# Two-layer encoder trunk: small parameters in two transfers, tables behind the first tokens, one norm placed late, softmax factors as reductions, residual rows requested half a tile sooner

## The chip, the cores and the metric

The kernel runs on one core of a Trainium2 chip. The core has a matrix engine (TensorE, "PE" in the profile; its weight loads are "PEld"), a vector engine (VectorE, "DVE"), a scalar engine for activations (ScalarE, "ACT"), a general engine (GpSimd, "POOL") and an engine that here only issues transfers (SyncE, "SP"). Each engine works through its own list of instructions in a fixed order and waits on semaphores for the others. Working memory is SBUF (128 partitions); matrix products land in eight PSUM banks. The metric is the device time of one execution in microseconds, the median of several runs.

## The reference

The input `x` has 2048 tokens of 1024 values, in float32, and goes through two layers.

```python
def even_layer(...):
    h = rms_norm(x, norm_g); proj = h @ w_in          # 1024 -> 3328
    aq, ak = apply_rope(rms_norm(aq), cos, sin), apply_rope(rms_norm(ak), cos, sin)
    ya = sliding_window_sink_attention(aq, ak, av, a_sinks) * silu(ag)
    yb = chunked_relbias_attention(rms_norm(bq), rms_norm(bk), bv, b_rel) * silu(bg)
    return x + concatenate([ya, yb]) @ w_out
def odd_layer(...):
    h = rms_norm(x, norm_g); q, k, v, gate = split(h @ w_in)   # 4 x 1024
    lam = exp(sum(lq1*lk1)) - exp(sum(lq2*lk2)) + lambda_init
    # per head, with the chunk-causal mask:
    a = softmax(q1 @ k1.T / 8) - lam * softmax(q2 @ k2.T / 8); o = a @ v
    o = rms_norm(o, subln_g) * (1 - lambda_init)
    return x + (o * silu(gate)) @ w_out
```

Beside the large weights there are many small parameters: norm gains of 64 values, eight sinks, four lambda vectors of 64 values, one gain of 128 values, and a table of relative biases of which the far ones are one value per head. The cosine and sine tables are worked out on the host and passed in.

## The kernel before

**Precision.** A product is taken as three matmuls with each operand split into a high and a low part (`mm3`, lines 212 to 217). So each weight chunk is copied to its high part by ACT (line 314), and POOL (at the very start also DVE) subtracts to get the low part (line 319). Hidden rows are split in the same way after their transposes (lines 347 and 348).

**Tiling.** Tokens go in 4 blocks of 512, each of 4 tiles of 128. `_project` runs once per layer, in two halves of two blocks. For each half, `hidden` is called for both blocks: it loads a tile of x (line 264), takes its mean square on ACT (line 333), the root on ACT and DVE (`rstd`, lines 205 to 209), scales the tile on DVE (line 338), transposes it on PE (line 343) and splits it. Then column groups of 512 are projected for both blocks. Tiles of x come from a pool with the tag `xt`, three buffers in layer 0 and four in layer 1. `mix0` is layer 0's attention with its output projection (`out_tile`, line 553 adds the residual), `mix1` is layer 1's.

**Start.** After the first block's `hidden`, `tables()` (line 272) calls `parameters` (line 154): fourteen small transfers on SP's queue, most of them broadcasts to 128 partitions, the four lambda vectors into a tile of the tag `xt`. Then it loads cosine and sine, in pieces of 32 values, and makes the four rotary tables on DVE (`rope_tables`, lines 187 to 195).

**Layer 1's attention.** For each head and block, `scores` makes rows of scores, at most 512 columns at a time (lines 977 and 978), their maximum (981) and exponentials with their sums (984). When a row has several chunks (nb > 1), lines 993 to 999 bring the chunks to one maximum and one sum, and line 1002 makes the factor of the second softmax, lambda in it. Then `combine` scales the second map on ACT (1016), the first on POOL (1017) and adds them on POOL (1018). `values` transposes the result (1032), copies it out of PSUM on DVE (1034) and multiplies with v (1036) into one PSUM bank (`pO`). `gate` copies that bank into a tile of the tag `ot` (1060). `projected` is the output projection; `out_begin` (1195) takes an `ot` tile for the residual rows and asks for them (1198), `out_end` adds them (1210) and stores (1211). The tag `ot` has four buffers.

**Order.** The program is traced in one order; a planner with a cost model then lays out each engine's list: of what is ready it takes what was traced first, and gives buffers of a pool as they come free. `issue_after(i)` makes what is traced inside it follow instruction i on i's engine only. `pace` weaves scores, values and side work (gates, output projection) by shares.

## Time and profile before

| what | us |
|---|---|
| median of 3 runs | 2771.64 (2765.45 to 2773.63) |
| the profiled execution's own time | 2771.11 |
| its span, first to last instruction | 2769.3 |
| PE busy | 2681.2 |
| DVE busy | 1768.0 |
| ACT busy | 1595.9 |
| POOL busy | 1438.4 |

The span is 1.8 us shorter than that execution's time. Layer 0's projections fill the first 600 us, its attention lasts to about 1160 us, layer 1's projections to about 1730 us, and the rest is layer 1's attention with its output projection. Matmuls overlap, so a row's length is more than the step from one to the next. A time in square brackets behind a row is the idle time of the engine before it, and what ended it.

### The profile page before, as it was taken

What the parts mean: (1) busy time and instruction counts of PE and PEld (TensorE: products, weight loads), DVE (VectorE), ACT (ScalarE), POOL (GpSimd) and SP (SyncE); (2) the same over time, 40 slices, a digit from 0 to 9 for tenths busy, and PEclk for the clock granted to TensorE, in tenths of its full rate; (3) what the DMA queues carried; (4) which work ended last, traced back from release to release, by engine and by line L of the source; (5) the groups of instructions that cost most, each with busy time, mean ns of one, the idle gap of its engine ahead of it and who ended that gap; (6) DMA issues with size and microseconds to landing.
All of it is one profiled execution on the core that took longest, in us unless ns stands there. A gap on an engine that the chain in (4) does not pass through costs nothing.

```text
span 2769.3 us, 43201 instructions
## 1 busy us (share of the span) xinstructions
PE 2681.2 (97%) x13384; PEld 2159.7 (78%) x13384; DVE 1768.0 (64%) x4397; ACT 1595.9 (58%) x3975; POOL 1438.4 (52%) x1595
## 2 busy tenths in 40 slices
PE   7999999999999999999999999999999999898999
PEld 6888888888788888788887888777777776676776
DVE  7642285337777777447833773478887787777772
ACT  5443544357867766333343332588887777776771
POOL 3651255245535354326553552467776666767661
PEclk9999999999999999999999999999999999999999
DMA  5774338557766656655486545887666656454542
GB/s 159 243 241 147 112 124 285 186 177 229 231 209 181 181 176 203 188 180 145 130 273 214 123 130 186 267 256 256 201 220 212 201 179 201 124 188 142 165 130 93
DMA packets 336373, 518.43 MB, mean 187 GB/s; under 512 B 36368, under 2 KB 128272, under 8 KB 336144
## 3 DMA queue, kind: packets, MB, share of 16 engines
q1 hardware_dynamic: 331536, 507.30, 58.2%
q10 hardware_dynamic: 4608, 8.39, 0.8%
q8 instruction: 106, 1.74, 0.3%
q14 instruction: 123, 1.01, 0.1%
HBM read 358.56 MB, written 157.02 MB: 186 GB/s over the span
## 4 chain that ended last, share of the span: by engine, by line
PE 80%; DVE 5%; ACT 4%; DMA 3%; issue 2%; POOL 1%; SPq 0%; ACTq 0%; DVEq 0%; POOLq 0%
PE cO L1036 8%; PE p1mm L215 6%; PE p1mm L216 6%; PE p1mm L217 6%; PE cS L977 4%; PE cS L978 4%; PE ctr L1032 4%; PE p0mm L217 3%; PE p0mm L216 3%; PE p0mm L215 3%; PE mom L215 2%; PE mom L217 2%; PE mom L216 2%; PE cG L215 2%; PE cG L216 2%; PE cG L217 2%
## 5 line engine op out<-in xcount | busy, mean ns | idle before, releaser
L984 ACT ACTIVATE cP<-cS,cnm 128x512 f32<-128x512 f32 (+3 forms) x640 | 395.4, 624 | 144.6 <-DVE cnm L981 131.8
L981 DVE TENSOR_REDUCE cnm<-cS 128x1 f32<-128x512 f32 (+3 forms) x640 | 373.5, 601 | 47.5 <-PE cS L978 41.3
L1018 POOL TENSOR_TENSOR cP<-cP,cP 128x512 f32<-128x512 f32 (+1 forms) x320 | 356.8, 1142 | 18.4 <-ACT cP L1016 18.3
L1017 POOL TENSOR_SCALAR cP<-cP,crl,cel 128x512 f32<-128x512 f32 (+3 forms) x288 | 209.9, 742 | 246.0 <-DVE crl L999 112.4
L319 POOL TENSOR_TENSOR p0wL<-p0ws,p0wH 128x256 fp32r<-128x256 f32 x264 | 192.6, 765 | 268.9 <-ACT p0wH L314 255.4
L215 PE MATMUL p1mm<-p1wH,p1hH 128*128 128x512 f32 x768 | 300.4, 393 | 0.8 <-ACT p1hH L347 0.8
L217 PE MATMUL p1mm<-p1wH,p1hL 128*128 128x512 f32 x768 | 300.1, 391 | 0.0
L216 PE MATMUL p1mm<-p1wL,p1hH 128*128 128x512 f32 x768 | 299.3, 390 | 0.0
L1036 PE MATMUL cO<-cpt,cv 128*128 128x512 f32 (+3 forms) x640 | 285.8, 532 | 9.1 <-DVE cpt L1034 8.7
L977 PE MATMUL cS<-ck,cqd 128*128 128x512 f32 (+3 forms) x640 | 261.1, 412 | 6.5 <-ACT cP L984 5.4
L1034 DVE COPY cpt<-ctr 128x512 f32<-128x512 f32 (+1 forms) x320 | 190.9, 605 | 101.3 <-PE ctr L1032 97.7
L215 PE MATMUL p0mm<-p0wH,p0hH 128*128 128x512 f32 (+1 forms) x640 | 238.6, 375 | 9.2 <-ACT p0wH L314 4.5
L216 PE MATMUL p0mm<-p0wL,p0hH 128*128 128x512 f32 (+1 forms) x640 | 238.7, 375 | 0.0
L217 PE MATMUL p0mm<-p0wH,p0hL 128*128 128x512 f32 (+1 forms) x640 | 237.4, 372 | 0.1
L978 PE MATMUL cS<-ck,cql 128*128 128x512 f32 (+3 forms) x640 | 232.8, 368 | 0.0
L1032 PEld LDWEIGHTS ctr<-ident,cP 128*128 128x128 f32 x1088 | 137.4, 141 | 118.0 <-issue 60.7
L319 POOL TENSOR_TENSOR p1wL<-p1ws,p1wH 128x512 fp32r<-128x512 f32 x112 | 153.2, 1392 | 139.1 <-ACT p1wH L314 113.4
L1016 ACT ACTIVATE cP<-cP,cc 128x512 f32<-128x512 f32 (+1 forms) x320 | 189.3, 654 | 17.1 <-DVE cc L1002 16.1
L1032 PE MATMUL ctr<-ident,cP 128*128 128x128 f32 x1088 | 175.6, 273 | 4.8 <-POOL cP L1018 4.1
L784 POOL TENSOR_SCALAR mPB<-mPB,mbr 128x640 f32<-128x640 f32 (+4 forms) x128 | 92.9, 740 | 150.6 <-DVE mbr L781 105.9
L215 PEld LDWEIGHTS p1mm<-p1wH,p1hH 128*128 128x128 f32 x768 | 144.3, 188 | 29.8 <-ACT p1hH L347 1.2
L217 PEld LDWEIGHTS p1mm<-p1wH,p1hL 128*128 128x128 f32 x768 | 144.2, 188 | 29.7
(315 smaller groups left out, 6919.0 us busy)
## 6 DMA issues: line engine op xcount, KB each, us to landing
ck<-ck SPq DMA_DIRECT2D x144, 256.0 KB, 4.6
cw<-wg SPq DMA_DIRECT2D x64, 512.0 KB, 5.3
p1ws<-in_od_w_in_dram SPq DMA_DIRECT2D x56, 512.0 KB, 3.9
p0ws<-in_ev_w_in_dram SPq DMA_DIRECT2D x48, 512.0 KB, 4.6
cv<-v SPq DMA_DIRECT2D x72, 256.0 KB, 4.2
cqd<-qH SPq DMA_DIRECT2D x32, 512.0 KB, 6.5
cql<-qL SPq DMA_DIRECT2D x32, 512.0 KB, 7.2
mks<-bk SPq DMA_DIRECT2D x24, 512.0 KB, 6.8
```

The lines of the kernel that those rows point to most:

```text
L215: mm(ps, aH, bH, start=first, stop=False)
L216: mm(ps, aH, bL, start=False, stop=False)
L217: mm(ps, aL, bH, start=False, stop=last)
L319: low.tensor_tensor(l[:, cs], ws[:, k, cs], f32(h[:, cs]), ALU.subtract)
L977: mm(ps, qd[:, m, js], kt[:, :wd], start=True, stop=False)
L978: self.anchor = mm(ps, ql[:, m, js], kt[:, :wd], start=False, stop=True).ins
L981: nc.vector.tensor_reduce(nm[:, m, z:z + 1], ps, AX.X, ALU.max, negate=True)
L984: exp = nc.scalar.activation(chunks[z][:, :wd], ps, AF.Exp, bias=nm[:, m, z:z + 1], accum_out=acc).ins
L1017: nc.gpsimd.tensor_scalar(p1, p1, rl[:, 0:1], e1, ALU.mult, ALU.mult)
L1018: nc.gpsimd.tensor_tensor(p1, p1, p2, ALU.add)
L1032: nc.tensor.transpose(turned[:, (j - j0) * P:(j - j0 + 1) * P], us[j][kt // 4][:, kk:kk + P], self.ident)
L1036: mm(O[:, j0 * P:], v, T[:, :wd], start=(kt == 0), stop=(kt == nkt - 1), skip_group_check=True)
```

## The change

It touches five places.

1. All gains, sinks, column parameters and the far biases are put into one array `given` of 128 rows on the host and come in one transfer; the four lambda vectors come in a second one. The fourteen transfers, and the one for the far biases in `mix0`, become two. Cosine and sine are laid out on the host as SBUF holds them, so that a partition gets one piece of 512 values.
2. In layer 0 `tables()` is put inside `issue_after(self.split)`: the DVE instructions of parameters and tables follow the last split of the first block's hidden rows.
3. In layer 1, first half, the second block's roots and scalings (DVE) follow the last residual addition of layer 0.
4. In `scores` the factors are kept in eight fixed tiles f with the slots sum, exponential, reciprocal, and (1, lambda factor). The maximum over chunks is written once per chunk by a reduction over a repeated view, and differences, the sum and the factor c2 become reductions along a slot axis. The number of DVE instructions for a row with several chunks stays six.
5. `projected` asks for the next output tile's residual rows when half of the present tile's products are issued.

```diff
@@ parameters
-        for n, g in zip(("ev_a_q_norm", "ev_a_k_norm", "od_q_norm", "od_k_norm"), norms):
-            nc.sync.dma_start(g, a[n].to_broadcast([P, HD]))
-        for i in range(2):
-            nc.sync.dma_start(gq[i * HD:(i + 1) * HD], a["ev_b_q_norm"].rearrange("o d -> d o"))
-            nc.sync.dma_start(gk[i * HD:(i + 1) * HD], a["ev_b_k_norm"].rearrange("o d -> d o"))
+        nc.sync.dma_start(g, a["given"])
         nc.vector.scalar_tensor_tensor(self.b_gain, gq, -0.125, gk, ALU.mult, ALU.mult)
-        nc.sync.dma_start(self.sink, a["ev_a_sinks"].to_broadcast([P, 8]))
-        for i, n in enumerate(("q1", "k1", "q2", "k2")):
-            nc.sync.dma_start(lv[:, i, :], a["od_lambda_" + n].to_broadcast([P, HD]))
+        nc.sync.dma_start(tmp[:, 0:4 * HD], a["lambdas"])
...
-        nc.sync.dma_start(self.sub, a["od_subln"].rearrange("o d -> d o"))
@@ tables
-            nc.sync.dma_start(self.cos, a["cos"].rearrange("(t p) d -> p t d", p=P))
-            nc.sync.dma_start(self.sin, a["sin"].rearrange("(t p) d -> p t d", p=P))
+            nc.sync.dma_start(self.cos.rearrange("p t d -> p (t d)"), a["cos"])
+            nc.sync.dma_start(self.sin.rearrange("p t d -> p (t d)"), a["sin"])
@@ hidden
-                r = self.rstd(sm, ss, 1, 1.0 / D, n + "x")
...
+                with tc.issue_after(behind) if behind is not None else nullcontext():
+                    r = self.rstd(sm, ss, 1, 1.0 / D, n + "x")
+                    for c in range(0, D, step):
+                        cs = slice(c, c + step)
+                        nc.vector.scalar_tensor_tensor(xt[:, cs], xt[:, cs], r, g_in[:, cs], ALU.mult, ALU.mult)
...
-                    nc.vector.tensor_tensor(oL, ps3, f32(oH), ALU.subtract)
+                    self.split = nc.vector.tensor_tensor(oL, ps3, f32(oH), ALU.subtract).ins
@@ _project
             if layer == 0 and not tabs:
-                tables()
-            h.append(hidden(blocks[1], 1))
+                with tc.issue_after(self.split):
+                    tables()
+            h.append(hidden(blocks[1], 1, behind=self.added if layer and not half else None))
@@ _mix1
+        for i in range(8):
+            f = fc.tile([P, 4, 2, 4], F32, tag=f"f{i}", name=n + f"f{i}")
+            nc.gpsimd.memset(f[:, 3, 0, :], 1.0)
+            nc.scalar.activation(f[:, 3, 1, :], f[:, 3, 0, :], AF.Copy, scale=self.nlam)
+            factors.append(f)
@@ scores
-                    nc.vector.tensor_reduce(top, nm[:, :, :nb], AX.X, ALU.min)
-                    nc.vector.tensor_tensor(below, nm[:, :, :nb], top.unsqueeze(2).to_broadcast([P, 2, nb]), ALU.subtract)
+                    nc.vector.tensor_reduce(nt[:, 1, :, :nb], again(nm[:, :, :nb], nb), AX.X, ALU.min, negate=True)
+                    nc.vector.tensor_reduce(below, nt[:, :, :, :nb].rearrange("p i m z -> p m z i"), AX.X, ALU.add)
                     nc.scalar.activation(e[:, :, :nb], below, AF.Exp, scale=-1.0)
-                    nc.vector.tensor_reduce(pe, el[:, :, :nb, :], AX.X, ALU.mult)
-                    nc.vector.tensor_reduce(l, pe, AX.X, ALU.add)
-                nc.vector.reciprocal(rl, l)
+                    nc.vector.tensor_reduce(pe, slots(0, 2), AX.X, ALU.mult)
+                    nc.vector.tensor_reduce(l[:, :, :nb], again(pe, nb), AX.X, ALU.add)
+                    nc.vector.reciprocal(rl[:, :, :nb], l[:, :, :nb])
+                else:
+                    nc.vector.reciprocal(rl[:, :, :1], la[:, :, :1])
                 c2 = small("c2", 4)[:, :nb]
-                if nb > 1:
-                    nc.vector.tensor_scalar(c2, e[:, 1, :nb], rl[:, 1:2], self.nlam, ALU.mult, ALU.mult)
-                else:
-                    nc.vector.tensor_scalar(c2, rl[:, 1:2], self.nlam, None, ALU.mult)
+                nc.vector.tensor_reduce(c2, slots(1 if nb > 1 else 2, 4)[:, 1], AX.X, ALU.mult)
@@ projected
-                    xr, ps, to = out_begin(b, j, c)
+                    tiles.pop(0)
+                    xr, ps, to = out_begin(b, j, c, xr=ready.pop())
                     for k in range(KT):
                         out_step(b, j, k, ps, room)
+                        if k == KT // 2:
+                            ready.append(residual(b, *tiles[0]) if tiles else None)
```

More of the change, by code (lines that the diff above doesn't have):

```diff
@@ L147, in constants @@
         nc.scalar.activation(self.ones, self.ident, AF.Copy, bias=1.0, scale=0.0)
-        self.small = [t(*x) for x in (
-            ("ev_a_q_norm", [P, HD]), ("ev_a_k_norm", [P, HD]), ("od_q_norm", [P, HD]), ("od_k_norm", [P, HD]),
-            ("bq_g", [P, 1]), ("bk_g", [P, 1]), ("b_gain", [P, 1]), ("sink", [P, 8]), ("nsink", [P, 8]),
-            ("nlam", [P, 1]), ("sub", [P, 1]),
-        )]
+        self.given = t("given", [P, 4 * HD + 19])
+        self.b_gain, self.nsink, self.nlam, self.sub = (
+            t(*x) for x in (("b_gain", [P, 1]), ("nsink", [P, 8]), ("nlam", [P, 1]), ("sub", [P, 1]))
+        )
     def parameters(self, tmp):
@@ L322, in weights_by, with hidden @@
                 yield
-        def hidden(b, i, between=(), early=None):
+        def hidden(b, i, between=(), early=None, behind=None):
             hH, hL = hidden_tile("H", i), hidden_tile("L", i)
@@ L936, in _mix1 @@
         hx = pool("hx", 3)
+        fc = pool("fc", 1)
+        factors = []
+        for i in range(8):
[3 more added lines that the diff above has]
+            factors.append(f)
         NS, NTR, NO, NM = self.BANKS1
@@ L1193, in gates, with residual @@
                 move()
-        def out_begin(b, j, c, pl=None, tag="S"):
+        def residual(b, j, c):
             rows, cols = slice((b * NTB + j) * P, (b * NTB + j + 1) * P), slice(c * 512, (c + 1) * 512)
@@ L1198, in out_begin @@
             nc.sync.dma_start(xr, self.x1[rows, cols])
+            return xr
+        def out_begin(b, j, c, pl=None, tag="S", xr=None):
+            rows, cols = slice((b * NTB + j) * P, (b * NTB + j + 1) * P), slice(c * 512, (c + 1) * 512)
+            xr = xr or residual(b, j, c)
             if b < NB - 1:
```

47 lines of the change are left out of this document (28 added, 19 removed).

## The prediction

> **What bounds the kernel now.** I read the page first, its busy times and its chain:
>
> ```profile
> PE 2681.2 (97%) x13384; PEld 2159.7 (78%) x13384; DVE 1768.0 (64%) x4397; ACT 1595.9 (58%) x3975; POOL 1438.4 (52%) x1595
> PE 80%; DVE 5%; ACT 4%; DMA 3%; issue 2%; POOL 1%; SPq 0%; ACTq 0%; DVEq 0%; POOLq 0%
> ```
>
> PE sets the end: idle for 2769.3 - 2681.2 = 88.1 us. The change takes no matmul away, so it can only win from these 88 us and from time in which PE runs at a lower clock after a pause. Next I read who made PE wait:
>
> ```profile
> PE p0trh L343 <- DVE p0xt L338: 9.6, 2, 7.5
> PE cO L1036 <- DVE cpt L1034: 8.7, 6, 3.8
> PE p0mm L215 <- ACT p0wH L314: 4.5, 1, 4.5
> PE com L215 <- DVE cxr L1210: 4.4, 2, 3.2
> PE mom L215 <- DVE mxr L553: 3.2, 1, 3.2
> ```
>
> Of the first row, 7.5 us is the wait for the very first tile, which no part of the change touches. The other 2.1 us and the four rows below (20.8 us) are where the five edits work. Last I read the timeline of each engine around these waits, and the clock in stretches.
>
> **Part 1 and 2, the start.** Here are POOL, SP, DVE, ACT and PE from 8 to 56 us, and the stretch 20 to 28 us (columns: stretch, length, busy time of PE, PEld, DVE, ACT, POOL with counts, granted clock, DMA share, GB/s).
>
> ```profile
> 8.69 3.41 POOL L319 TENSOR_TENSOR p0wL<-p0ws,p0wH 128x256 fp32r<-128x256 f32 x4 [7.39 <-ACT p0wH L314]
> 13.22 0.47 SPq L165 DMA_DIRECT2D bk_g<-in_ev_b_k_norm_dram  x1
> 13.86 0.45 SPq L308 DMA_DIRECT2D p0ws<-in_ev_w_in_dram  x1
> 18.59 2.79 SPq L278 DMA_DIRECT2D p0sin<-in_sin_dram  x1
> 19.08 0.16 DVE L166 SCALAR_TENSOR_TENSOR b_gain<-bq_g,bk_g 128x1 f32<-128x1 f32 x1 [4.41 <-DMA bk_g<-in_ev_b_k_norm_dram]
> 20.20 1.15 ACT L314 ACTIVATE p0wH<-p0ws 128x512 fp32r<-128x512 f32 x2 [5.21 <-DMA p0ws<-in_ev_w_in_dram]
> 20.89 0.79 PE L215 MATMUL p0mm<-p0wH,p0hH 128*128 128x512 f32 x1 [4.51 <-ACT p0wH L314]
> 20.00:28.00 8.00, 7.09 (x25) 5.83 (x26) 7.96 (x14) 4.85 (x10) 2.45 (x2) 0.57 0.92 169
> 24.03 0.68 DVE L187 TENSOR_TENSOR p0tqC<-p0cos,ev_a_q_norm 128x512 f32<-128x512 f32 x1
> 37.35 0.15 DVE L174 SCALAR_TENSOR_TENSOR nlam<-p0tmp 128x1 f32<-128x1 f32 x1
> 37.52 24.63 SPq L264 DMA_DIRECT2D p0xt<-in_x_dram  x6
> 55.29 1.06 PE L343 MATMUL p0trh<-ident,p0xt 128*128 128x128 f32 x8 [2.13 <-DVE p0xt L338]
> ```
>
> Three things hang together. The last quarter of the first weights is issued at 13.86, behind eight small transfers (the last at 13.22), and lands at 20.20; PE has nothing to do for 4.51 us. DVE meanwhile stands 4.41 us at b_gain, with the second tile's norm queued behind it. After the pause PE runs at 0.57 of its clock for 7.09 us busy, which costs 7.09 x 0.43 = 3.0 us more. Then the lambda vectors hold one of three `xt` buffers until 37.35, and the next x tile is asked for right after, at 37.52; its late norm is part of the 2.13 us at 55.29.
>
> After the change one transfer stands where eight stood, so the weights can go as soon as their buffer is free (an estimate: POOL's four pieces take 3.41 us from 8.69, the first buffer's two end near 10.4, so some 3 us before 13.86), and cosine and sine, whose sine issue alone held SP for 2.79 us, come as 512-value pieces. DVE no longer has b_gain ahead of the norm: it is behind the first block's last split. That is a new wait. Queued behind it are twelve table instructions and the lambda chain, and the first to wait for them are the rotary steps of the first group; PE then has the first block's four projected tiles to work on, and before, the tables began no sooner than 24.03 either. The lambda buffer comes free right behind the split rather than at 37.35. The sum's ceiling is 4.51 + 3.0 + 2.13 = 9.6 us. I take **8**, since the fourth tile's x has to come behind the weights. Bounds: 9.6 won, and 2 lost if the late tables leave the norm of the second block as late again (the 2.13 us wait, doubled).
>
> **Part 3, from layer 0 to layer 1.**
>
> ```profile
> 1120.69 1.27 DVE L207 SCALAR_TENSOR_TENSOR p1xu<-p1xss,p1xy 128x1 f32<-128x1 f32 x1 [4.94 <-ACT p1xy L206]
> 1122.45 2.35 DVE L338 SCALAR_TENSOR_TENSOR p1xt<-p1xt,p1xr,p1g_in 128x1024 f32<-128x1024 f32 x1
> 1124.83 1.29 DVE L553 TENSOR_TENSOR mxr<-mom,mxr 128x512 f32<-128x512 f32 x2
> 1125.58 0.50 PE L215 MATMUL mom<-mw,myH 128*128 128x512 f32 x1 [3.25 <-DVE mxr L553]
> 1125.00:1130.00 5.00, 4.42 (x12) 3.50 (x13) 3.79 (x6) 0.00 (x0) 2.17 (x2) 0.66 0.70 198
> ```
>
> DVE waits 4.94 us for the second block's first norm, with two residual additions (L553) behind it in its list; both PSUM banks of the output projection are full and PE stops for 3.25 us, then runs 4.42 us at 0.66, which costs 1.5 us. With the norms behind the last addition nothing stands ahead of L553, and 4.75 us go. What is late next: two scalings of the second block now come after the last addition, where the first block's splits are due. The splits were traced first, so the planner takes them when they are ready; a scaling that starts just ahead costs PE at most one such instruction. PE's cover is the first block's projection, 4 tiles of 24 matmuls. I take **4**; bounds 4.75 won, and, if both scalings (2 x 2.35 at worst) land ahead of the splits, nothing won.
>
> **Part 4, the factors.** The small DVE instructions between maximum and combination, min/median/max in ns, and the two places where they stop PE:
>
> ```profile
> L993 DVE TENSOR_REDUCE ctop<-cnm x96: 133/152/163, 1742.8 to 2693.0; 128x2 f32<-128x4 f32 x32, 128x2 f32<-128x6 f32 x32, 128x2 f32<-128x8 f32 x32
> L995 DVE TENSOR_TENSOR cbelow<-cnm,ctop x96: 139/166/3271, 1743.0 to 2693.2; 128x4 f32<-128x4 f32 x32, 128x6 f32<-128x6 f32 x32, 128x8 f32<-128x8 f32 x32
> L997 DVE TENSOR_REDUCE cpe<-cel x96: 140/156/172, 1743.5 to 2694.2; 128x4 f32<-128x8 f32 x32, 128x6 f32<-128x12 f32 x32, 128x8 f32<-128x16 f32 x32
> L1002 DVE TENSOR_SCALAR cc<-cel,crl,nlam x96: 179/289/4042, 1744.7 to 2694.8; 128x2 f32<-128x2 f32 x32, 128x3 f32<-128x3 f32 x32, 128x4 f32<-128x4 f32 x32
> 2400.31 3.27 DVE L995 TENSOR_TENSOR cbelow<-cnm,ctop 128x8 f32<-128x8 f32 x1
> 2405.57 1.12 PE L1036 MATMUL cO<-cpt,cv 128*128 128x512 f32 x2 [1.67 <-DVE cpt L1034]
> 2554.37 4.04 DVE L1002 TENSOR_SCALAR cc<-cel,crl,nlam 128x4 f32<-128x4 f32 x1
> 2550.92 5.00 POOL L1018 TENSOR_TENSOR cP<-cP,cP 128x512 f32<-128x512 f32 x4
> 2559.05 1.12 PE L1036 MATMUL cO<-cpt,cv 128*128 128x512 f32 x2 [3.82 <-DVE cpt L1034]
> 2555.00:2565.00 10.00, 6.18 (x16) 3.08 (x16) 6.04 (x7) 1.57 (x3) 8.51 (x9) 0.83 0.20 52
> ```
>
> The reductions never exceed 172 ns in 192 instructions; the two-input subtraction and the scaling reach 3271 and 4042 ns on eight or four elements. The 4.04 us begin inside a run of four POOL additions, so I read it as DVE waiting for POOL, in a form of instruction that the reductions don't have. The change makes both of them reductions. New sizes (up to 32 elements read) aren't in the trace; from L993 to L997 twice the input costs 4 ns in the median, so I price all six at 0.16 us. Counted in DVE time each row with several chunks then wins at least (0.166 + 0.289) - 0.32 = 0.13 us, and the outliers go. In PE time it is the two waits, 3.82 + 1.67, and the slow clock after the first, 6.18 x 0.17 = 1.05: 6.5 us. I take **5.5**, because another two-input instruction may meet the same POOL run. Bounds: 0, and the whole 8.7 us of that wait row plus 1.05. The sixteen instructions that fill the f tiles lie on POOL and ACT ahead of the stage and cost nothing; uncovered, 16 x 0.2 = 3 us.
>
> The Trainium skill ("VectorE: DVE Perf Modes", section "Rules for kernel authors") speaks against this edit: expect `tensor_reduce` at the lowest mode, the slowest DVE operation, and restructure. By that rule this part would win nothing and the forecast would be 5.5 us higher; the medians above, 152 and 156 ns against 166 and 289, say otherwise at these sizes. The same notes ("SBUF — State Buffer", "SBUF: two separate sides") say that DVE with two SBUF inputs and POOL take a shared port pair exclusively and for one whole instruction. If so, a wait ends after one POOL addition, 5.00 / 4 = 1.25 us, the two waits would be worth 2.5 us and not 5.5, and the forecast would be 3 us higher; the 4.04 us row spans three of them, so here the measured wait is longer than the rule's.
>
> **Part 5, residual rows.**
>
> ```profile
> PE cO L1036 <- ACT cot L1060: 0.5, 1, 0.5
> 2387.27 0.61 ACT L1060 ACTIVATE cot<-cO 128x512 f32<-128x512 f32 x1
> 2387.61 1.51 SPq L1198 DMA_DIRECT2D cxr<-x  x3
> 2393.72 0.69 DVE L1210 TENSOR_TENSOR cxr<-com,cxr 128x512 f32<-128x512 f32 x1 [2.31 <-DMA cxr<-x]
> 2394.47 0.50 PE L215 MATMUL com<-p1hH,cy 128*128 128x512 f32 x1 [3.24 <-DVE cxr L1210]
> 2495.84 0.51 PE L215 MATMUL com<-p1hH,cy 128*128 128x512 f32 x1 [1.19 <-DVE cxr L1210]
> ```
>
> Requests come three at a time, 0.34 us behind the copy into another `ot` tile: the planner gave the buffers in the order traced, and the rows of the tile in work came 6 us late. Asked for half a tile sooner, the first of each bunch can stand ahead of that copy. PE's ceiling is 3.24 + 1.19 = 4.4 us. The price is a buffer held longer. I take **2.5**, between all and a little over none; bounds 4.4 won, 4 lost (the wait doubled the other way).
>
> **The sum.** 8 + 4 + 5.5 + 2.5 = 20 us. Every list is laid out anew, and the old layout's waits were not planned either; I charge one new wait of the size of the L553 row, 3 us. So 17 us less than the profiled execution's own 2771.1: **2754 us**. That execution lies 0.5 us under the median of the three runs, so no correction.
>
> **Rivals.** (B) *The waits only move.* Another two-input DVE instruction meets POOL and the requests stay behind the copy: parts 4 and 5 win nothing. Or the reductions cost PE what they save. For it: L207's row of 1.27 us, on one element, shows the same stretch in another instruction. Against it: the instructions that part 4 leaves are the same in number as before. Time 2771 - 12 + 3 = 2762. The rule of the Trainium skill on reductions, quoted under part 4, leads here too. (C) *The start gives nothing*, because the fourth tile or the late tables take the place of the weights: 2771 - 12 + 3 = 2762 as well, by 4 + 5.5 + 2.5. Against it: the 4.51 us have one cause in the rows. (D) *The new layout costs what the edits win*, 17 us of new waits more: about 2771. (E) *Slower: the residual tile takes the `ot` buffer that the copy L1060 needs.* That copy empties the one PSUM bank of the values; if it waits, PE's next product waits. Each time costs about the 3.24 us row. There are 16 heads in the last two blocks; from 17 / 3.24, so 6 of them, the gain is gone, and if it strikes ten, 2754 + 32 = 2786. For it: three requests at a time leave one of the four buffers. Against it: that is so before the change too, and PE waited only 0.5 us for that copy in all.
>
> **How the numbers follow.** Forecast 0.55; B 0.13; C 0.08; D 0.14; E 0.10. About 0.3%, 8.3 us, is what a measurement of this kernel can tell from no change: 2763 and 2780 are the edges. The forecast with its own spread (2743 to 2763) and most of B and C are faster (0.74), D and the rest within (0.17), most of E slower (0.09). Range 2740 to 2769: below, the sum with the ceilings 9.6 + 4.75 + 9.75 + 4.4 = 28.5 and no charge would be 2743, with a little for shortened small waits; above, it stops just short of D.
>
> **What would show it.** Start: the last quarter of the weights issued near 11 us, no PE wait over 2 us before 60 us, PE's clock not at a half between 20 and 28. Boundary: L553 no later than 1.5 us behind its last matmul. Factors: no instruction in the place of L995 and L1002 over 0.2 us, and the row of waits for L1034 shorter by 5 us. Residual rows: a request more than 10 us ahead of its addition. I am wrong if these hold and the end stays above 2763, or if PE's waits on the copy L1060 grow beyond 5 us.

## The result, and the profile after

The changed kernel takes 2755.9 us (median of six runs, 2753.0 to 2757.9) where the kernel before, run beside it, takes 2772.6: a ratio of 0.9948, 95% interval 0.9934 to 0.9962. The forecast was 2754. The profiled execution took 2753.4 us, with a span of 2751.6. So the total came out as forecast; its terms did not, and most of what follows is about that.

The engines' busy times and the chain that ended last, from the page of the changed kernel:

```profile
PE 2677.6 (97%) x13384; PEld 2160.1 (79%) x13384; DVE 1736.5 (63%) x4397; ACT 1594.6 (58%) x3983; POOL 1434.7 (52%) x1603
PE 84%; DMA 5%; DVE 5%; ACT 3%; issue 2%; POOL 1%; SPq 0%; ACTq 0%; DVEq 0%; POOLq 0%
```

PE is idle for 2751.6 - 2677.6 = 74.0 us, 14.1 less than before; the other 3.6 us of the span's 17.7 are busy time of the same 13384 matmuls. The mean granted clock is 0.996 in both executions, too coarse a figure to say where these 3.6 us come from. VectorE is busy for 31.5 us less. Who made PE wait (waited in total, times, longest):

```profile
PE p0trh L337 <- DVE p0xt L332: 13.7, 4, 7.5
PE cS L980 <- ACT cP L987: 10.2, 13, 1.6
PE cO L1039 <- DVE cpt L1037: 2.1, 5, 0.7
PE p1mm L208 <- ACT p1hH L341: 2.0, 1, 2.0
PE com L208 <- ACT cot L1063: 0.7, 1, 0.7
PE mom L208 <- DVE mxr L548: 0.6, 1, 0.6
```

Four of the five waits that the prediction named are gone or small: on the weights (4.5 us before), on the values' copy cpt (8.7, now 2.1), on cxr (4.4, none now), on mxr (3.2, now 0.6). The wait for the copy into cot, on which rival E rested, is 0.7 us. Two rows grew: the first tiles, 9.6 to 13.7, and the scores waiting for ScalarE's exponentials, 5.4 before and 10.2 now.

To see where in the run the time went, take four marks that every version has: the first score matmul of layer 0 (tile mSA), its last output matmul (mom), the first score matmul of the last attention (cS), and the end of the span. A group's row gives the times of its first and last instruction. Before:

```profile
L642 PE MATMUL mSA<-mksA,mqd x128: 219/283/385, 599.5 to 1066.5; 128*128 128x256 f32 x120, 128*128 128x128 f32 x8
L217 PE MATMUL mom<-mw,myL x256: 387/393/628, 748.8 to 1159.7; 128*128 128x512 f32 x128
L977 PE MATMUL cS<-ck,cqd x640: 218/397/799, 1729.0 to 2691.2; 128*128 128x512 f32 x136, 128*128 128x128 f32 x8, 128*128 128x384 f32 x8, 128*128 128x256 f32 x8
```

and after:

```profile
L636 PE MATMUL mSA<-mksA,mqd x128: 218/282/385, 596.9 to 1061.4; 128*128 128x256 f32 x120, 128*128 128x128 f32 x8
L210 PE MATMUL mom<-mw,myL x256: 387/393/481, 744.2 to 1150.2; 128*128 128x512 f32 x128
L980 PE MATMUL cS<-ck,cqd x640: 218/395/800, 1721.1 to 2673.3; 128*128 128x512 f32 x136, 128*128 128x128 f32 x8, 128*128 128x384 f32 x8, 128*128 128x256 f32 x8
```

Differences of these marks give four stages. The same rows of every version that was run give this table (us; the stages are of one profiled execution each, the median and the ratio are of several runs, against runs of the kernel before on the same chip, whose medians were 2769.7 to 2774.5; what the versions are stands below):

| version | median | ratio, 95% interval | projection of layer 0 | its attention and output | projection of layer 1 | last attention and output |
|---|---|---|---|---|---|---|
| before | 2772.6 | 1 | 599.5 | 560.2 | 569.3 | 1040.3 |
| changed | 2755.9 | 0.9948 (0.9934 to 0.9962) | 596.9 | 553.3 | 570.9 | 1030.5 |
| tables_free | 2758.7 | 0.9963 (0.9950 to 0.9976) | 599.8 | 553.7 | 570.3 | 1032.2 |
| norm_not_behind | 2757.3 | 0.9961 (0.9947 to 0.9975) | 596.1 | 560.4 | 569.8 | 1029.5 |
| factors_as_before | 2770.2 | 0.9999 (0.9991 to 1.0008) | 598.4 | 551.3 | 569.5 | 1050.0 |
| rows_not_sooner | 2754.7 | 0.9943 (0.9931 to 0.9956) | 595.9 | 554.0 | 570.8 | 1034.0 |
| folds_alone | 2762.9 | 0.9975 (0.9964 to 0.9985) | 602.8 | 556.7 | 569.3 | 1030.9 |
| no_folds_no_rows | 2762.8 | 0.9968 (0.9957 to 0.9979) | 599.5 | 551.6 | 568.8 | 1040.4 |
| extra_two_input | 2779.0 | 1.0026 (1.0014 to 1.0039) | 597.5 | 554.8 | 569.4 | 1053.7 |
| extra_reduction | 2756.5 | 0.9946 (0.9930 to 0.9962) | 597.6 | 556.7 | 570.7 | 1035.8 |
| rstd_folds | 2740.1 | 0.9876 (0.9858 to 0.9893) | 585.9 | 556.1 | 566.4 | 1033.1 |
| tables_one_pass | 2753.6 | 0.9928 (0.9912 to 0.9944) | 592.6 | 552.4 | 570.0 | 1032.4 |
| gate_psum | 2743.9 | 0.9894 (0.9880 to 0.9908) | 598.4 | 555.1 | 568.3 | 1019.3 |
| all_three | 2727.7 | 0.9854 (0.9838 to 0.9871) | 583.8 | 555.3 | 565.9 | 1020.3 |

How finely may one read it? Eight versions have the changed kernel's first stage, but for the fills of the f tiles (changed, norm_not_behind, factors_as_before, rows_not_sooner, no_folds_no_rows, the two with an instruction more, gate_psum), and lie between 595.9 and 599.5 there. So 3 to 4 us in one stage of one execution say little, and 8 us a great deal. The kernel before spreads as much: folds_alone has its start, and took 602.8 where it took 599.5.

From before to after: 2.6 us came from the start (forecast 8), 6.9 from the stage that ends at the boundary, 1.6, no more than the spread, were given back behind it (together 5.3, forecast 4), and 9.8 came from the last attention (forecast 5.5 + 2.5 = 8).

**The start.** The weights do go sooner. But here is what stands on VectorE, POOL and PE 20 to 40 us later (start, duration, engine, line, what; in brackets the idle time ahead and what ended it):

```profile
10.52 0.38 SPq L301 DMA_DIRECT2D p0ws<-in_ev_w_in_dram  x1
32.50 0.69 DVE L180 TENSOR_TENSOR p0tqC<-p0cos,given 128x512 f32<-128x512 f32 x1
40.71 0.43 DVE L186 TENSOR_SCALAR p0tkS<-p0tkS 128x512 f32<-128x512 f32 x1
42.89 2.63 POOL L386 TENSOR_TENSOR p0xn<-p0xn,p0tqC 128x512 f32<-128x512 f32 x2 [16.74 <-DVE p0t L382]
45.49 2.49 POOL L388 TENSOR_TENSOR p0xn<-p0xn,p0t 128x512 f32<-128x512 f32 x2
43.05 1.33 DVE L201 SCALAR_TENSOR_TENSOR p0xu<-p0xu,p0xy 128x1 f32<-128x1 f32 x2
44.30 1.25 DVE L200 SCALAR_TENSOR_TENSOR p0q8u<-p0qss,p0q8y 128x8 f32<-128x8 f32 x1
45.48 1.29 DVE L202 SCALAR_TENSOR_TENSOR p0xr<-p0xu,p0xy 128x1 f32<-128x1 f32 x2
46.77 1.23 DVE L201 SCALAR_TENSOR_TENSOR p0q8u<-p0q8u,p0q8y 128x8 f32<-128x8 f32 x1
47.92 2.47 DVE L332 SCALAR_TENSOR_TENSOR p0xt<-p0xt,p0xr,p0g_in 128x1024 f32<-128x1024 f32 x2
49.34 3.65 PE L337 MATMUL p0trh<-ident,p0xt 128*128 128x128 f32 x16 [5.49 <-DVE p0xt L332]
```

and the stretch 48 to 52 us (busy time of PE, PEld, VectorE, ScalarE, POOL with counts, granted clock, DMA share, GB/s):

```profile
48.00:52.00 4.00, 2.66 (x13) 2.69 (x14) 4.00 (x9) 1.19 (x2) 0.00 (x0) 0.50 0.00 0
```

The tables, with a few splits and reductions between them, fill VectorE from 32.5 to 41.1 us. Then, in each of the four rows from 43.05 to 46.77, one tiny instruction, on one or eight elements, takes some 1.2 us (the rows of two hold a short one as well), and each row ends when one of POOL's four rotary operations ends. The second block's norm is issued behind them, and PE, which had run ahead, waits 5.49 us and then runs at half clock. By 44 us PE had been busy for 35.5 us and had begun 160 matmuls (the 100th at 30.9 us), against 31.1 us and 125 (the 100th at 38.8) before the change; by 60 us it is 46.2 us and 206 against 44.4 us and 191. So the start had won about what was forecast, and lost most of it between 44 and 60 us.

**The boundary.** VectorE's last residual additions, the first small steps of the second block's norm, and PE's first product of layer 1:

```profile
1116.90 1.29 DVE L548 TENSOR_TENSOR mxr<-mom,mxr 128x512 f32<-128x512 f32 x2 [6.38 <-PE mom L210]
1152.36 0.22 DVE L200 SCALAR_TENSOR_TENSOR p1xu<-p1xss,p1xy 128x1 f32<-128x1 f32 x2
1152.55 0.47 PE L208 MATMUL p1mm<-p1wH,p1hH 128*128 128x512 f32 x1 [1.97 <-ACT p1hH L341]
```

The two additions that had stood behind the norm now follow their matmuls at once, and the norms sit among the first block's splits. PE's first wait in layer 1 is 1.97 us where it was 0.8. That it comes from the norm's new place is not shown: it ends with a copy of ScalarE, and in four other versions that hold the norm back in the same way (tables_free, factors_as_before, tables_one_pass, gate_psum) it is 0.8 us.

**The factors.** The reductions that took the places of the old forms (min/median/max in ns):

```profile
L998 DVE TENSOR_REDUCE cnt<-cnt x96: 133/172/188, 1735.0 to 2675.1; 128x4 f32<-128x8 f32 x32, 128x6 f32<-128x18 f32 x32, 128x8 f32<-128x32 f32 x32
L999 DVE TENSOR_REDUCE cbelow<-cnt x96: 136/163/172, 1735.2 to 2675.3; 128x4 f32<-128x8 f32 x32, 128x6 f32<-128x12 f32 x32, 128x8 f32<-128x16 f32 x32
L1007 DVE TENSOR_REDUCE cc<-cf x128: 125/155/169, 1723.5 to 2676.7; 128x1 f32<-128x2 f32 x32, 128x2 f32<-128x6 f32 x32, 128x3 f32<-128x9 f32 x32, 128x4 f32<-128x12 f32 x32
```

None is over 0.2 us, where the old subtraction and scaling reached 3.27 and 4.04. The same holds for the whole trace of the changed kernel: in 21 groups of VectorE instructions (by line, tile and shape) the longest is over 0.3 us above the group's median, and all 21 are `tensor_tensor` or `scalar_tensor_tensor` on inputs in SBUF; none of the 1281 reductions is among them. The old scaling (L1002) was stretched too, though it has one tensor and two columns of factors as inputs; which property of it does that was not tried.

### The profile page after: what moved, and what is told of

It is laid out like the page before. It is cut to its first block, busy times and chain, and to the rows that moved or that the text cites. A ratio compares the mean times of both kernels' runs of the same rounds, so it can differ in the third digit from the quotient of the medians.

```text
span 2751.6 us, 43191 instructions
## 1 busy us (share of the span) xinstructions
PE 2677.6 (97%) x13384; PEld 2160.1 (79%) x13384; DVE 1736.5 (63%) x4397; ACT 1594.6 (58%) x3983; POOL 1434.7 (52%) x1603
## 3 DMA queue, kind: packets, MB, share of 16 engines
q1 hardware_dynamic: 322240, 507.30, 58.4%
## 4 chain that ended last, share of the span: by engine, by line
PE 84%; DMA 5%; DVE 5%; ACT 3%; issue 2%; POOL 1%; SPq 0%; ACTq 0%; DVEq 0%; POOLq 0%
PE cO L1039 8%; PE p1mm L208 6%; PE p1mm L209 6%; PE p1mm L210 6%; PE cS L980 4%; PE cS L981 4%; PE ctr L1035 4%; PE p0mm L209 3%; PE p0mm L208 3%; PE p0mm L210 3%; PE mom L208 2%; PE mom L210 2%; PE mom L209 2%; PE cG L208 2%; PE cG L209 2%; PE cG L210 2%
## 5 line engine op out<-in xcount | busy, mean ns | idle before, releaser
L987 ACT ACTIVATE cP<-cS,cnt 128x512 f32<-128x512 f32 (+3 forms) x640 | 395.1, 622 | 145.0 <-DVE cnt L984 125.6
L984 DVE TENSOR_REDUCE cnt<-cS 128x1 f32<-128x512 f32 (+3 forms) x640 | 374.5, 601 | 57.8 <-PE cS L981 51.1
L1020 POOL TENSOR_SCALAR cP<-cP,cf 128x512 f32<-128x512 f32 (+1 forms) x320 | 227.2, 722 | 295.8 <-DVE cc L1007 102.6
L1021 POOL TENSOR_TENSOR cP<-cP,cP 128x512 f32<-128x512 f32 (+1 forms) x320 | 357.9, 1146 | 17.3 <-ACT cP L1019 17.2
L209 PE MATMUL p1mm<-p1wL,p1hH 128*128 128x512 f32 x768 | 300.0, 391 | 0.0
L980 PE MATMUL cS<-ck,cqd 128*128 128x512 f32 (+3 forms) x640 | 260.7, 411 | 11.1 <-ACT cP L987 10.2
L209 PE MATMUL p0mm<-p0wL,p0hH 128*128 128x512 f32 (+1 forms) x640 | 239.1, 376 | 0.2 <-POOL p0wL L312 0.2
L1019 ACT ACTIVATE cP<-cP,cc 128x512 f32<-128x512 f32 (+1 forms) x320 | 188.9, 652 | 17.7 <-DVE cc L1007 17.5
L208 PEld LDWEIGHTS p1mm<-p1wH,p1hH 128*128 128x128 f32 x768 | 144.7, 188 | 30.9 <-ACT p1hH L341 2.4
```

The costliest lines, as they stand in the source:

```text
L208: mm(ps, aH, bH, start=first, stop=False)
L209: mm(ps, aH, bL, start=False, stop=False)
L980: mm(ps, qd[:, m, js], kt[:, :wd], start=True, stop=False)
L984: nc.vector.tensor_reduce(nm[:, m, z:z + 1], ps, AX.X, ALU.max, negate=True)
L987: exp = nc.scalar.activation(chunks[z][:, :wd], ps, AF.Exp, bias=nm[:, m, z:z + 1], accum_out=acc).ins
L1020: nc.gpsimd.tensor_scalar(p1, p1, rl[:, 0, 0:1], e1, ALU.mult, ALU.mult)
```

## The experiments: each part undone

Four versions of the changed kernel, each with one part put back.

**The tables without their wait (tables_free).**

```diff
-                with tc.issue_after(self.split):
-                    tables()
+                tables()
```

> The changed kernel, with only the wait of the layer 0 tables taken out (they may go as soon as their data is there). Theory: the late tables fill VectorE from 32 to 41 us, the norms of the second block come behind them, and this is PE's new 5.49 us wait at 49 us. Then that wait is under 2 us here and the end 3 to 5 us earlier than in the changed kernel: 0.9930 of the kernel before where the changed one is 0.9948 (about 2751 us). Rival: VectorE has as much to do in the first 60 us in either order, and the wait only stands elsewhere: within 2 us of the changed kernel, 0.9941 to 0.9955. Second rival: the tables then stand ahead of the first tiles' norms: 3 us slower or more, 0.9959.

Measured: 0.9963, some 4 us behind the changed kernel's 0.9948, with intervals that overlap. The wait at 49 us is gone as the theory said, but PE meets two others. PE and POOL of this version:

```profile
21.55 0.72 PE L209 MATMUL p0mm<-p0wL,p0hH 128*128 128x512 f32 x1 [4.01 <-POOL p0wL L312]
26.36 3.70 PE L337 MATMUL p0trh<-ident,p0xt 128*128 128x128 f32 x16 [2.38 <-DVE p0xt L332]
17.07 9.82 POOL L312 TENSOR_TENSOR p0wL<-p0ws,p0wH 128x256 fp32r<-128x256 f32 x6 [2.76 <-ACT p0wH L307]
```

The theory falls, and the second rival holds in kind: earlier tables stand ahead of the first tiles. They also slow POOL. Its six weight splits take 9.82 / 6 = 1.64 us each beside VectorE's table products and norms; the median of that line's 264 splits in this version is 0.74. So VectorE and POOL hold each other up, in both directions.

**The norm not held back (norm_not_behind).**

```diff
-            h.append(hidden(blocks[1], 1, behind=self.added if layer and not half else None))
+            h.append(hidden(blocks[1], 1))
```

> The changed kernel without the wait of the second block's norms for the last residual addition at the boundary of the layers. Theory by the two traces: 4.3 us were won up to the last output product, 2.8 of them given back in the next 50 us because norms and splits of two blocks now share VectorE, so undoing it costs 1.5 us: 0.9953 (2757 to 2758 us), and PE's wait for the residual addition is back at 3 us. Rival, the forecast's own term: 4 us slower, 0.9962. Second rival: the wait gives back all it wins, 0.9948.

Measured: 0.9961, 3.6 us behind the changed kernel (0.0013 x 2772), between the theory's 1.5 and the rival's 4; the intervals overlap, so the ratio alone doesn't decide between them. The trace shows the mechanism: PE's wait for the addition is back, and the stage to the last mom takes 560.4 us, as before the change, against 553.3.

```profile
PE mom L208 <- DVE mxr L548: 3.3, 1, 3.3
```

**The factors as before (factors_as_before).**

```diff
-                    nc.vector.tensor_reduce(below, nt[:, :, :, :nb].rearrange("p i m z -> p m z i"), AX.X, ALU.add)
+                    nc.vector.tensor_tensor(below, nm[:, :, :nb], top.unsqueeze(2).to_broadcast([P, 2, nb]), ALU.subtract)
...
-                nc.vector.tensor_reduce(c2, slots(1 if nb > 1 else 2, 4)[:, 1], AX.X, ALU.mult)
+                    nc.vector.tensor_scalar(c2, e[:, 1, :nb], rl[:, 1:2], self.nlam, ALU.mult, ALU.mult)
```

> The changed kernel with the factors of the last attention computed as before (subtraction of two inputs, scaling by two columns; no f tiles). Theory: VectorE's small two-input instructions are held up by POOL's additions, the reductions are not, so the old forms again show single instructions of over 1 us, and the end is 5.5 to 8 us later: 0.9968 to 0.9977. Rival: the gain of the attention stage came from the residual rows and the new layout of the lists, the small instructions lie off PE's path: within 2 us of the changed kernel, 0.9941 to 0.9955.

Measured: 0.9999. Undoing this one part loses the whole gain, twice what the theory said: the last attention takes 1050.0 us, 19.5 more than in the changed kernel and 9.7 more than before the change. Not all of this is waiting: in that stretch PE is busy for 1016.6 us with the same matmuls, against 1005.4, at a granted clock of 0.98 against 1.00, so 11.2 us are slower matmuls and 8.3 are idle time. The long instructions are back:

```profile
L989 DVE TENSOR_TENSOR cbelow<-cnm,ctop x96: 140/166/4427, 1733.2 to 2693.1; 128x4 f32<-128x4 f32 x32, 128x6 f32<-128x6 f32 x32, 128x8 f32<-128x8 f32 x32
L996 DVE TENSOR_SCALAR cc<-cel,crl,nlam x96: 179/290/3898, 1734.9 to 2694.7; 128x2 f32<-128x2 f32 x32, 128x3 f32<-128x3 f32 x32, 128x4 f32<-128x4 f32 x32
```

**The rows asked for as before (rows_not_sooner).**

```diff
-                    xr, ps, to = out_begin(b, j, c, xr=ready.pop())
+                    xr, ps, to = out_begin(b, j, c)
...
-                        if k == KT // 2:
-                            ready.append(residual(b, *tiles[0]) if tiles else None)
```

> The changed kernel with the residual rows asked for at the start of their own tile, as before. Theory: requests stand in bunches behind the copy of the values again, PE waits 3 to 4.4 us for the residual addition in the last two blocks, end 2.5 to 4.4 us later: 0.9957 to 0.9964. Rival: the order of the requests came from the layout of the other parts and stays good: within 1.5 us, 0.9943 to 0.9953.

Measured: 0.9943 (0.9931 to 0.9956), no difference from the changed kernel that the runs can tell: the rival's number. A gain of 2.5 us could hide in these intervals, and the last attention of the profiled execution is 3.5 us longer here. Yet the theory's wait is back. PE's waits in this version:

```profile
PE cS L980 <- ACT cP L987: 6.2, 11, 1.5
PE com L208 <- DVE cxr L1218: 3.8, 2, 2.6
```

With the rows asked for sooner the 3.8 us are gone and PE's wait for the exponentials is 10.2 instead of 6.2. So part 5 took waits away and as much came up elsewhere. At the place of the longest one, the row of this version and then PE's and ScalarE's rows of the changed kernel:

```profile
2386.38 0.49 PE L208 MATMUL com<-p1hH,cy 128*128 128x512 f32 x1 [2.62 <-DVE cxr L1218]
```

```profile
2383.78 0.50 PE L980 MATMUL cS<-ck,cqd 128*128 128x512 f32 x1 [1.37 <-ACT cP L987]
2385.44 0.63 ACT L1104 ACTIVATE cy<-coy 128x512 fp32r<-128x512 f32 x1 [1.71 <-DMA coy<-o]
2386.79 0.50 PE L980 MATMUL cS<-ck,cqd 128*128 128x512 f32 x1 [1.57 <-ACT cP L987]
```

A PE that does not pause for 2.62 us reaches the exponentials sooner and pauses there for 1.37 + 1.57 us. Ahead of the second of these ScalarE itself stood 1.71 us for a transfer, behind which the exponentials were queued. The same exchange of totals stands between folds_alone (3.5 for cxr, 6.0 for the exponentials) and the changed kernel.

## The experiments: which part gives what, and by what cause

**The reductions alone on the kernel before (folds_alone)**, the factor part of the diff and nothing else:

```diff
+                factors.append(factors.pop(0))
+                f = factors[-1]
+                la, e, rl = f[:, 0], f[:, 1], f[:, 2]
...
+                nc.vector.tensor_reduce(c2, slots(1 if nb > 1 else 2, 4)[:, 1], AX.X, ALU.mult)
```

> The kernel before with the change's factors as reductions and nothing else of the change. From the traces the last attention (1700 us to the end) took 10.0 us less in the changed kernel than before, and 19.7 us less than in the changed kernel with the old factors. Theory: the reductions are worth what the stage won from before to after, 10 us: ratio 0.9964. Rival, the forecast's own size, the two waits of PE that could be seen: 5.5 us, 0.998. Second rival, the size that undoing them showed: 15 to 20 us, 0.993 to 0.9945.

Measured: 0.9975, which is 6.9 us (4.2 to 10.0 by the interval). The last attention falls from 1040.3 to 1030.9. Both the theory (10) and the forecast's size (5.5) lie in the interval or at its edge; 15 to 20 do not.

**Neither reductions nor rows sooner (no_folds_no_rows)**, the edits of factors_as_before and rows_not_sooner together.

> The changed kernel with the old factors and the old requests for the residual rows (so the start and the boundary alone are changed). With the old factors alone the kernel was 10 us ahead at 1600 us and lost all of it in the last attention. Theory: asking sooner for the rows costs this when the small instructions are held up; without it the 10 us stay: 0.9964. Rival: in any order of the lists but the one of before, the old factors meet POOL's additions at worse places, and the loss stays: 0.9985 to 1.001.

Measured: 0.9968, 2762.8 us. The theory holds: with the old factors, asking for the rows sooner costs 0.9999 - 0.9968, 8.6 us (last attention 1040.4 against 1050.0); with the reductions it costs and gives nothing. And the two parts at the start and the boundary are worth 0.0032 x 2772 = 8.9 us by themselves, where the forecast said 12. Most of the 9.6 us by which the two last attentions differ is slower matmuls (busy 1016.6 against 1009.8 us, idle 33.4 against 30.6). Why sooner rows hurt beside the old factors was not tried; it is not the rival E of the prediction, since PE waits 1.1 us in all for the copy into `cot` there.

**One small instruction more, in two forms (extra_two_input, extra_reduction).** Its result is read by nobody; 96 of them run in the last attention.

```diff
+                    nc.vector.tensor_tensor(more, nm[:, :, :nb], nm[:, :, :nb], ALU.subtract)
```

> The changed kernel with one more small VectorE instruction per row of several chunks (96 in all), a subtraction of two inputs of up to 8 elements whose result nobody reads. It measures the disputed cost by itself. Theory: a two-input form waits for POOL's running operation, so some of the 96 last 0.6 to 4 us, their sum is 30 to 40 us instead of 15, and the end is 4 to 12 us later than in the changed kernel: 0.9962 to 0.999. Rival: it is only an instruction more on an engine that is 63% busy: within 2 us of the changed kernel and of the run with a reduction more.

```diff
+                    nc.vector.tensor_reduce(more, nt[:, :, :, :nb].rearrange("p i m z -> p m z i"), AX.X, ALU.add)
```

> The changed kernel with one more small VectorE instruction per row of several chunks (96 in all), a reduction over pairs of the same size, whose result nobody reads: the partner of the run with a subtraction more. Theory: none of the 96 is over 0.2 us, their sum is 15 us of VectorE's time, and the end is within 2 us of the changed kernel: 0.9941 to 0.9955. Rival: the number of small instructions counts, not their form: as late as the run with the subtraction.

Measured: the subtraction costs 1.0026 - 0.9948, 22 us, where the theory said 4 to 12; the reduction costs nothing that the runs can tell (0.9946, 0.9930 to 0.9962). Same number, same place, same result size: this pair speaks most clearly for the form. One thing besides the form differs, since the planner lays out the lists anew: read off the traces, 1364 of PE's 13384 matmuls stand at another place than in the changed kernel with the subtraction (by at most 30 places), 131 with the reduction. How much of the 22 us is layout was not separated. What is the form's own is VectorE's time, 58.4 us for the 96 subtractions and 15.0 for the 96 reductions. The subtraction's row:

```profile
L1010 DVE TENSOR_TENSOR cmore<-cnt x96: 137/158/4640, 1735.8 to 2698.4; 128x4 f32<-128x4 f32 x32, 128x6 f32<-128x6 f32 x32, 128x8 f32<-128x8 f32 x32
```

PE's largest row of waits in that version, and then one of the 96 with POOL beside it on the timeline:

```profile
PE cO L1042 <- DVE cpt L1040: 14.7, 7, 4.0
```

```profile
2383.42 4.64 DVE L1010 TENSOR_TENSOR cmore<-cnt 128x8 f32<-128x8 f32 x1
2380.72 4.78 POOL L1024 TENSOR_TENSOR cP<-cP,cP 128x512 f32<-128x512 f32 x4
2385.45 2.58 POOL L1108 TENSOR_TENSOR cy<-coy,cy 128x512 fp32r<-128x512 f32 x2
```

and the reduction's:

```profile
L1010 DVE TENSOR_REDUCE cmore<-cnt x96: 131/156/166, 1739.2 to 2683.7; 128x4 f32<-128x8 f32 x32, 128x6 f32<-128x12 f32 x32, 128x8 f32<-128x16 f32 x32
```

The subtraction of eight elements begins at 2383.42, inside an unbroken run of six POOL operations, and ends at 2388.06, when the run does (2385.45 + 2.58 = 2388.03). The median, 158 ns, is about that of the reduction (156). A median hides this cost, the maximum shows it. The long wait is the exception: of the 116 VectorE instructions on at most 16 elements that took over 0.6 us in this trace, every one ends within 0.25 us of the end of a POOL operation; 106 overlap one such operation, six overlap two and four overlap four.

## The experiments: the same cause elsewhere

If two-input forms are held up by POOL, three other places of the changed kernel should gain from other forms.

**The refinement of the reciprocal roots (rstd_folds)**, the helper whose lines L200 to L202 stood in front of the second block's norm:

```diff
-        nc.vector.scalar_tensor_tensor(u, ss, EPS / scale, y0, ALU.add, ALU.mult)
-        nc.vector.scalar_tensor_tensor(u, u, -0.5 * scale, y0, ALU.mult, ALU.mult)
-        nc.vector.scalar_tensor_tensor(r, u, 1.5, y0, ALU.add, ALU.mult)
+        nc.vector.tensor_reduce(u, f, AX.X, ALU.mult)
+        nc.scalar.activation(f[:, :, 0], u, AF.Copy, bias=1.5, scale=-0.5 * scale)
+        nc.vector.tensor_reduce(r, f[:, :, 0:2], AX.X, ALU.mult)
```

(f holds the sum of squares and twice the first root, both written by ScalarE.) Beside the form, this takes one of three VectorE instructions away.

> The changed kernel with the refinement of every reciprocal root (three small VectorE instructions of two inputs, the helper of lines 198 to 202) done by two reductions and two steps of ScalarE more. In the changed kernel the norms of the second block stood from 43.05 to 47.92 us behind four of these instructions of 1.2 to 1.3 us, while POOL had four rotary operations of 1.25 us, and PE then waited 5.49 us. Theory: that is what gave the start's gain back; the wait falls to about 1 us, and with the slow clock behind it the end is 4 to 7 us earlier: 0.9923 to 0.9934. Rival: VectorE is full from 32 to 60 us in any case (the tables), the norm only waits for something else: within 2 us of the changed kernel. Second rival: the longer chain over ScalarE costs PE at each group: 2 us later or more, 0.9955.

Measured: 0.9876, 2740.1 us, some 16 to 20 us ahead of the changed kernel by median and by ratio, and 10 by the two spans; more than the theory's 4 to 7. The larger group of its new reductions, and then PE's waits in the place of the 5.49 us:

```profile
L202 DVE TENSOR_REDUCE p0q8u<-p0q8f x48: 160/177/180, 28.4 to 499.8; 128x8 f32<-128x24 f32 x48
```

```profile
47.86 1.06 PE L339 MATMUL p0trh<-ident,p0xt 128*128 128x128 f32 x8 [1.63 <-DVE p0xt L334]
50.08 1.06 PE L339 MATMUL p0trh<-ident,p0xt 128*128 128x128 f32 x8 [1.16 <-DVE p0xt L334]
```

Layer 0's projection ends 11.0 us sooner (585.9 against 596.9). Of these, some 4.7 us lie between 40 and 60 us: PE is idle there for 3.28 us instead of 5.48, and its granted clock is 1.00 where it was 0.83, which had cost 14.52 x 0.17 = 2.5 us. That is the size of the theory, although VectorE is as full as before in that stretch (busy for all of the 20.00 us in both). The rest comes later, from the same helper at the column groups: in the changed kernel 45 of its 144 instructions on eight elements in layer 0 take over 0.3 us longer than their median.

**Tables in one pass (tables_one_pass)**, each product with its scale in one instruction of two inputs:

```diff
-        if scale != 1.0:
-            v.tensor_scalar(C, C, scale, None, ALU.mult)
...
+                v.scalar_tensor_tensor(to, x, k, g(lo), ALU.mult, ALU.mult)
```

> The changed kernel with the scale of the rotary tables folded into their products, so that four passes of VectorE at 38.7 to 41.1 us (0.69 + 0.42 + 0.42 + 0.43 = 1.96 us), and five in layer 1, fall away. Theory of a full VectorE: everything behind the tables comes 2 us sooner, PE's wait of 5.49 us at 49 us is 3.5 us, end 2 to 4 us earlier than in the changed kernel: 0.9934 to 0.9941. Rival: the wait is set by POOL's rotary operations, which move with the tables: within 1.5 us.

Measured: 0.9928, with an interval that overlaps the changed kernel's; layer 0's projection 592.6 us, 4.3 sooner, and PE's wait is 3.39 us, close to the 3.5 expected. By the trace the theory of a full VectorE holds for its 2 us, beside the stretched instructions.

```profile
47.70 3.13 PE L339 MATMUL p0trh<-ident,p0xt 128*128 128x128 f32 x16 [3.39 <-DVE p0xt L334]
```

**The gate's two large instructions with one input in PSUM (gate_psum).**

```diff
-                    nc.scalar.activation(sq, ms, AF.Ln, bias=self.eps, scale=1.0 / P)
-                nc.vector.scalar_tensor_tensor(sg, sq, 0.5, sg, ALU.mult, ALU.add)
-                nc.scalar.activation(sg, sg, AF.Exp, scale=-1.0)
-                nc.vector.scalar_tensor_tensor(o, o, self.sub, sg, ALU.mult, ALU.mult)
+                    nc.scalar.activation(ms, ms, AF.Ln, bias=self.eps, scale=1.0 / P)
+                nc.vector.scalar_tensor_tensor(sg, ms, 0.5, sg, ALU.mult, ALU.add)
+                nc.scalar.activation(ms, sg, AF.Exp, scale=-1.0)
+                nc.vector.scalar_tensor_tensor(o, o, self.sub, ms, ALU.mult, ALU.mult)
```

> The changed kernel with the two large VectorE instructions of the output gate (lines 1077 and 1079, 32 each, up to 2.59 us where 0.7 is usual) reading one of their inputs from PSUM instead of SBUF. Theory: VectorE forms with one PSUM input are not held up by POOL (the residual additions never exceed 0.70 us), so the two lines keep to 0.8 us, and the last attention gains 1 to 4 us: 0.9934 to 0.9945. Rival: the PSUM bank of the sum of squares is held some 2 us longer, and the transposes that share its banks wait: 1 to 5 us later, 0.9952 to 0.9966.

Measured: 0.9894, and the last attention takes 1019.3 us, 11.2 less than in the changed kernel; again more than expected, and no sign of the rival's waits on the bank. Its page, and then the two lines (up to 2290 and 2589 ns in the changed kernel):

```profile
PE 2673.7 (98%) x13384; PEld 2158.6 (79%) x13384; DVE 1719.9 (63%) x4397; ACT 1594.6 (58%) x3983; POOL 1417.8 (52%) x1603
```

```profile
L1077 DVE SCALAR_TENSOR_TENSOR csg<-cms,csg x32: 639/680/694, 1775.6 to 2721.8; 128x512 f32<-128x512 f32 x32
L1079 DVE SCALAR_TENSOR_TENSOR cot<-cot,sub,cms x32: 665/740/751, 1777.3 to 2723.3; 128x512 f32<-128x512 f32 x32
```

VectorE is busy for 16.6 us less, and POOL, with the same 1603 instructions, for 16.9 less, in its scalings and additions of the maps (L1020 and L1021). How much of the gain came through POOL was not separated.

**All three together (all_three).**

> The changed kernel with the three last edits together: reciprocal roots by reductions, scaled rotary tables in one pass, output gate with one PSUM input. Theory: they hold in different places. By the stages, roots won 13 us up to 1700 us and little behind it, the gate won 10.4 us behind 1700 us only, and the tables' 5 us lie in the first 300 us, where roots won 6.3 of theirs already; so from the changed kernel's 0.9948, 0.0072 by the roots, 0.0054 by the gate and none to 0.0020 by the tables: 0.9802 to 0.9822, 2718 to 2725 us. Rival: the gains share one cause, PE's waits that any new order of the lists moves, and do not add: 0.985 to 0.9875, no better than the best of the three alone.

Measured: 0.9854 (0.9838 to 0.9871), 2727.7 us; better than each of the three by the median, short of the sum that was expected, and inside the range of the rival (0.985 to 0.9875), so the ratio does not refute it. The expected sum was taken from ratios of different groups of runs. By the spans of the profiled executions the three won 10.1, 10.5 and 4.2 us, 24.8 in sum, and 26.3 together, which speaks for adding; these are single executions. By the stages too they add: 583.8 and 565.9 in the projections are those of the roots with 2.1 and 0.5 us more won, and 1020.3 is that of the gate. This version takes 1.46% less than the kernel before, some 40 us. PE is now idle for 2725.3 - 2666.4 = 58.9 us.

```profile
PE 2666.4 (98%) x13384; PEld 2154.4 (79%) x13384; DVE 1631.7 (60%) x4261; ACT 1626.4 (60%) x4239; POOL 1418.5 (52%) x1603
```

## Why the prediction was right in sum, and where its steps failed

**The start: forecast 8 us, found 2.6 (0 to 3.6 in the eight versions with this start, up to 6.9 against folds_alone).** All that was said of the old waits' cause holds: the last quarter of the weights is issued at 10.52 us ("near 11"), the 4.51 us wait is gone, the clock between 20 and 28 is full. The mark "no PE wait over 2 us before 60 us" failed, by the 5.49 us at 49.34. The step that failed is "the first to wait for them are the rotary steps of the first group", and with it the bound of 2 us for a late norm: queued behind the tables was also the second block's norm, and between the two came four small two-input instructions that POOL's rotary operations stretched to 1.25 us each, some 4.5 us. Where 2.13 us of waiting and 2 more were allowed for, the wait took 5.49 us and the slow clock 2.5. The prediction had this very mechanism in hand in part 4 and in rival B, and priced it for the last attention only. Rival C had the outcome (the start gives little, through the late tables), but tables_free shows that the lateness as such is not at fault: early tables cost as much elsewhere. rstd_folds took the stretched instructions away and found 4.7 us of it between 40 and 60 us; its other 6.3 us in that stage were no part of the forecast.

**The boundary: forecast 4, found 3.6 by the ratios of norm_not_behind (intervals overlapping) and 5.3 by the stages.** The mechanism is the one given. What was named as late next, the second block's scalings, now stands behind the last addition as was said; that it cost PE anything is not shown.

**The factors: forecast 5.5, found 6.9 (folds_alone), 6.9 again between no_folds_no_rows and rows_not_sooner (0.9968 - 0.9943).** Right in mechanism and nearly in size: both marks hold (nothing over 0.2 us in the place of the old forms, the row of waits for cpt down by 6.6 us), and the last attention fell by 9.4 and 6.4 us. The doubt that made 5.5 of 6.5 ("another two-input instruction may meet the same POOL run") was not needed. What the prediction could not see is that the size depends on the company: beside the sooner rows the old factors cost 0.9999 - 0.9948, 14 us, and of the 19.5 us in the last attention 11.2 are slower matmuls.

**The residual rows: forecast 2.5, found none that the runs can tell.** The wait for cxr went as forecast (4.4 us to none), and of the 32 requests, each paired with its addition in order, 26 stand more than 10 us ahead, where 22 did. The step that failed is that PE's idle time for a wait is won when the wait goes. By the traces it went into the next wait, for the exponentials, 6.2 to 10.2 us. That is rival B's clause for part 5 by outcome, though not by its cause (the requests did move).

**One new wait, charged at 3 us.** The layout brought one of 5.49 us with a slow clock behind it; it belongs to the first point.

So 8 + 4 + 5.5 + 2.5 - 3 = 17 met 17 us with 2.6, 5.3 and 9.8 by the stages. The sum was better than its terms: the start's loss was made up by parts that gave a little more each. That it met the result within a microsecond or two is luck.

**The rules weighed in part 4.** The Trainium skill ("VectorE: DVE Perf Modes", section "Rules for kernel authors") would have kept the factors out of reductions; extra_reduction shows 96 reductions more at no cost that can be told, so at these sizes the measurement decides against it. The other rule of the Trainium skill ("SBUF — State Buffer", section "Who interferes with whom") says that a VectorE instruction with two SBUF inputs contends with POOL's reads, that one with at most one SBUF input outside the two-port modes does not, and that `tensor_reduce` never does on this chip. The runs agree: 22 us against none for the extra pair, 694 and 751 ns at most with one input in PSUM, and no reduction among the 21 stretched groups. Had the prediction priced every small two-input instruction by it, and not only the two that the change touched, it would have looked at L207 to L209 in the start.

## What to carry to other kernels

Where POOL works beside VectorE, look at the maximum of every small VectorE instruction with two SBUF inputs, not at its median, and ask which engine stands behind the longest ones; a reduction over neighbouring slots, or one input in PSUM, does the same work without the wait. A wait that is taken from the busiest engine is won only as far as the next engine is ahead: look at the second row of the waits before counting it. When transfers are sped up at the start, follow the same tile to its next queue.

## What the runs showed of the hardware that was not expected

- A small two-input VectorE instruction may wait through a whole run of POOL operations, 4.64 us on eight elements, and not just for the one that is running; far more often (106 of 116 in that trace), and in the start, the two engines took turns, one operation of some 1.25 us each time. What decides between the two was not found.
- It works both ways: POOL's weight splits took 1.64 us beside VectorE's table products, with a median of 0.74 over the run, and POOL's busy time fell by 16.9 us when two VectorE lines read PSUM.
- 96 instructions whose result nobody reads, with a median of 0.158 us, cost 22 us, the lists' new layout included.
- Undoing a part can cost more in slower matmuls than in waiting: undoing the factors added 8.3 us of idle time to the last attention and 11.2 us to the busy time of the same matmuls, at a granted clock of 0.98 against 1.00.
